# A transformer layer on one core: the last head's turn, the modulation sums and one row load get written places

## The chip, the cores and the metric

The kernel runs on one core of a Trainium2 chip. The metric is the device time of one execution in microseconds. A core has five engines that run side by side, each through its own list of instructions in order: TensorE (PE in the profile, matmuls into PSUM banks), VectorE (DVE), ScalarE (ACT), GpSimd (POOL) and SyncE (SP). Loads and stores are issued by SP and by ScalarE, each in the order of that engine's list.

## The reference

One layer of a hybrid decoder, for one sequence of 512 positions and 1024 channels, all in float32. A conditioning vector `c` gives six modulation vectors (`mod = silu(c) @ ada_w + ada_b`: shift, scale and gate of the mixer, and the same of the feed-forward part). What matters here is the end of the mixer and the start of the feed-forward part:

```python
h = rms_norm(h, ml_norm_g[l].reshape(H, Dh)).reshape(Bsz, S, D_ML)
h = (h * jax.nn.sigmoid(o_pre.astype(jnp.float32))).astype(x.dtype)
...
mix = jnp.concatenate([h, y], axis=-1) @ w_out[l]
x = x + g1 * rms_norm(mix, mix_post_g[l])
u = rms_norm(x, ffn_pre_g[l]) * (1.0 + sc2) + sh2
up = causal_dwconv(u @ ffn_up[l], ffn_conv_w[l], ffn_conv_b[l])
```

`h` are the outputs of four attention-like heads of 256 channels, `y` those of a convolution; `w_out` is the output projection, 2048 to 1024.

## The kernel before, in words

Channels are cut into tiles of 128 (one to a partition), the 512 positions into four tiles of 128. Every float32 product is made as three matmuls of split operands: a value is cut into a rounded part (`...h`) by a copy on ScalarE and a remainder (`...l`) by a subtraction on POOL (line 207, `w_split`; some on VectorE), and high x high, low x high and high x low are summed in PSUM (line 225, `mm3`). Weights come into two rotating buffers (`raws`), so the load of a weight waits until POOL has split the weight two loads earlier.

**The output projection** is done in two halves of 512 columns. The first half sums into the banks `mixa0` to `mixa3` (one for each position tile), the second into `mixb0` to `mixb3`. Three of the four heads go by a scheme of fewer products on 2 x 2 blocks (`mix_product`, with weight sums `mt1` to `mt4` and parts `m11`, `m21`, `m22`, and the results put together by VectorE: `mku`, and the updates of `mixb`); the ten pieces of `PLAIN` (the convolution's eight, and the last head's two as pieces 8 and 9) go directly (`wo0_n` for the first half, `wo1_n` for the second). The last head's outputs are turned (transposed on TensorE into `hT`), and split into `hh` by ScalarE (line 701) and `hl` by VectorE (line 702); pieces 8 and 9 need them.

**What sets the order.** TensorE and SP run in the order in which the program is written. On VectorE, ScalarE and POOL a scheduler orders the instructions by a model of time and by priority (`tc.cur_priority += LATER` makes a block less urgent), unless they stand in a block `with in_order()`, which keeps the three engines in written order, or unless one is tied behind another (`behind`, an order without a wait for data).

**The modulation sums.** `ada_block(i, ...)` loads row block i of the modulation weights (512 KB, `adaT`, issued on ScalarE) and sums its product with the condition on VectorE (line 189, `junk<-ada`, `junk<-wide` or `junk<-spare` by the buffer). I call them row i and sum i. Sums 16 to 23 give the gate of the mixer: `gain` makes the post-norm row from it, `send_rows` turns it on TensorE (`gT`), copies it (`gTs`, line 798) and writes it to DRAM (`row_d`, issued on ScalarE), and `row` loads it back into every partition (`wide<-row_d`, into the buffer that row 30 used before, issued on SP). Sums 24 to 39 give scale and shift of the feed-forward part.

**The chain behind the projection** (`chain_sums`, `chain_x`, `chain_u`), for each position tile: the sum of squares of both halves, `rm0t` on VectorE, a power on POOL, the new x, its squares, another power, the scaled `un`, and the transposes `xT` on TensorE, from which the first matmuls of the feed-forward part (`up`) get their operand. VectorE takes up the splits of the first up weight (`wup_0l` ... `wup_1536l`) just ahead of that.

## Time and profile before

| | us |
|---|---|
| median of the runs (three: 774.85, 775.5, 776.74) | 775.5 |
| the profiled execution | 776.75 |
| its span, first to last instruction | 775.0 |
| TensorE busy | 757.6 (98%) |
| VectorE busy | 580.1 (75%) |
| GpSimd busy | 547.3 (71%) |
| ScalarE busy | 427.7 (55%) |
| mean granted TensorE clock | 0.991 |

In the rows of a timeline the first number is the start in us from the start of the span, the second the time taken, then engine, line, operation and tiles (out<-in; the buffer numbers are left out, so `wo_8` stands for `wo0_8` and `wo1_8`). What stands in square brackets is the idle time of the engine before the instruction, and what ended it. A matmul's time covers its way through the array; what it costs TensorE is the distance to the next start.

### The profile page before, as it was taken

To read this page: it belongs to the slowest core of one execution; us is meant where nothing else is said; L and a number is where in the kernel's file an instruction comes from. 1 tells how busy PE (TensorE), PEld (TensorE's weight loads), DVE (VectorE), ACT (ScalarE), POOL (GpSimd) and SP (SyncE) were. 2 spreads that over 40 slices of the span, in tenths; PEclk is the share of its full clock that TensorE was granted. 3 is DMA by queue.
4 is the path that set the end of the run, shared out by engine and by line. 5 is a ranking of instruction groups with operands and counts; after the bars stand their busy time and mean duration, and the time that the engine had idled before them with its cause. 6 is when DMAs were issued, how large, how long until landed. Compare 5 with 4: busy or idle time off the path is not lost.

```text
span 775.0 us, 10264 instructions
## 1 busy us (share of the span) xinstructions
PE 757.6 (98%) x3485; PEld 626.6 (81%) x3485; DVE 580.1 (75%) x862; ACT 427.7 (55%) x823; POOL 547.3 (71%) x447
## 2 busy tenths in 40 slices
PE   7999999999999999999899999999999999999996
PEld 5878898878788788788678988888888888888885
DVE  6669999979689796488697878775765578654548
ACT  6675429784766656573347643443444345566633
POOL 5779849995685763858751066986988686599944
PEclk9999999999999999999899999999999999999999
DMA  8994954311140341855673755756586584896363
GB/s 316 343 389 160 184 148 129 128 70 56 54 135 30 126 170 45 278 208 206 230 257 126 246 222 184 295 229 236 206 303 227 185 295 157 298 397 244 105 239 141
DMA packets 41976, 154.92 MB, mean 200 GB/s; under 512 B 3954, under 2 KB 5378, under 8 KB 32772
## 3 DMA queue, kind: packets, MB, share of 16 engines
q1 hardware_dynamic: 28052, 101.57, 36.6%
q10 hardware_dynamic: 12272, 49.56, 17.6%
q0 software_dynamic: 1600, 3.15, 2.4%
q8 instruction: 27, 0.44, 0.2%
q14 instruction: 25, 0.20, 0.1%
HBM read 134.19 MB, written 26.35 MB: 207 GB/s over the span
## 4 chain that ended last, share of the span: by engine, by line
PE 87%; DVE 4%; DMA 3%; issue 2%; ACT 2%; POOL 1%; DVEq 0%; SPq 0%; POOLq 0%; ACTq 0%
PE up L225 31%; PE dn L225 13%; PE qko L225 13%; PE vo L225 8%; PE glu L225 7%; PE glu L362 4%; PE s L648 2%; PE o L659 2%; DVE junk L189 2%; PE v L225 1%; PE mixb L225 1%; DMA mt<-mixq 1%; PE mixa L225 1%; DMA wglu<-in_w_glu 1%; DMA wo<-in_w_out 1%
## 5 line engine op out<-in xcount | busy, mean ns | idle before, releaser
L911 DVE SCALAR_TENSOR_TENSOR cv<-gt,cvw,cv 128x502 f32<-128x502 f32 (+23 forms) x200 | 136.7, 729 | 2.7 <-ACT cv L899 1.6
L907 POOL TENSOR_TENSOR cs<-cs,cs 128x510 f32<-128x510 f32 (+3 forms) x32 | 41.9, 1308 | 1.3 <-ACT cs L905 1.0
L189 DVE SCALAR_TENSOR_TENSOR junk<-ada,cb 128x1024 bf16<-128x1024 f32 x21 | 35.6, 1696 | 5.9 <-DMA ada<-in_adaT 5.6
L207 POOL TENSOR_TENSOR wup_0l<-wup,wup_0h 128x512 fp32r<-128x512 f32 x18 | 26.0, 1444 | 17.2 <-ACT wup_0h L206 17.2
L225 PE MATMUL up<-u2h,wup_1024h 128*128 128x512 f32 (+1 forms) x96 | 35.8, 373 | 0.0
L225 PE MATMUL up<-u2h,wup_0h 128*128 128x512 f32 (+1 forms) x96 | 35.7, 372 | 0.0
L225 PE MATMUL up<-u2l,wup_512h 128*128 128x512 f32 (+1 forms) x96 | 35.7, 372 | 0.0
L225 PE MATMUL up<-u2l,wup_0h 128*128 128x512 f32 (+1 forms) x96 | 35.7, 372 | 0.0
L225 PE MATMUL up<-u2h,wup_0l 128*128 128x512 f32 (+1 forms) x96 | 35.7, 372 | 0.0
L225 PE MATMUL up<-u2h,wup_512l 128*128 128x512 f32 (+1 forms) x96 | 35.7, 371 | 0.0
L225 PE MATMUL up<-u2h,wup_1536l 128*128 128x512 f32 (+1 forms) x96 | 35.6, 371 | 0.0
L225 PE MATMUL up<-u2h,wup_1536h 128*128 128x512 f32 (+1 forms) x96 | 35.6, 371 | 0.0
L225 PE MATMUL up<-u2l,wup_1536h 128*128 128x512 f32 (+1 forms) x96 | 35.6, 371 | 0.0
L225 PE MATMUL up<-u2h,wup_512h 128*128 128x512 f32 (+1 forms) x96 | 35.6, 371 | 0.0
L225 PE MATMUL up<-u2l,wup_1024h 128*128 128x512 f32 (+1 forms) x96 | 35.6, 371 | 0.0
L225 PE MATMUL up<-u2h,wup_1024l 128*128 128x512 f32 (+1 forms) x96 | 35.6, 371 | 0.0
L905 ACT ACTIVATE cs<-gt,cvw 128x511 f32<-128x511 f32 (+4 forms) x40 | 27.0, 712 | 7.7 <-POOL cs L907 4.7
L207 POOL TENSOR_TENSOR wup_1536l<-wup,wup_1536h 128x512 fp32r<-128x512 f32 x18 | 24.2, 1347 | 7.5 <-ACT wup_1536h L206 7.0
L1383 POOL TENSOR_TENSOR b<-b 128x512 f32<-128x512 f32 x11 | 14.7, 1334 | 18.3 <-DVE b L1382 16.0
L342 DVE SCALAR_TENSOR_TENSOR junk<-ada,cps 128x1024 bf16<-128x1024 f32 x16 | 19.5, 1220 | 9.5 <-DMA ada<-in_adaT 8.7
L1384 DVE TENSOR_TENSOR b<-b 128x512 f32<-128x512 f32 x11 | 19.4, 1761 | 9.5 <-POOL b L1383 9.5
L207 POOL TENSOR_TENSOR wup_512l<-wup,wup_512h 128x512 fp32r<-128x512 f32 x18 | 25.3, 1403 | 0.0
(1263 smaller groups left out, 2785.6 us busy)
## 6 DMA issues: line engine op xcount, KB each, us to landing
wup<-in_w_up SPq DMA_DIRECT2D x22, 1024.0 KB, 5.4
b<-in_w_down ACTq DMA_DIRECT2D x11, 1024.0 KB, 7.1
spill_t<-b ACTq DMA_DIRECT2D x11, 1024.0 KB, 4.2
ada<-in_adaT ACTq DMA_DIRECT2D x21, 512.0 KB, 6.4
wqko<-in_w_qko SPq DMA_DIRECT2D x9, 1024.0 KB, 4.8
ada<-in_adaT SPq DMA_DIRECT2D x16, 512.0 KB, 7.3
wvo<-in_w_vo SPq DMA_DIRECT2D x6, 1024.0 KB, 4.8
wglu<-in_w_glu SPq DMA_DIRECT2D x5, 1024.0 KB, 8.9
```

The costliest lines, as they stand in the source:

```text
L189: t = V.scalar_tensor_tensor(out=junk, in0=r, scalar=1.0, in1=cb, op0=ALU.mult, op1=ALU.mult, accum_out=mod[:, i : i + 1])
L207: last_w[0] = (eng or G).tensor_tensor(out=lo[:, :n], in0=src, in1=hi[:, :n].bitcast(F32), op=ALU.subtract)
L225: PE.matmul(ps, l, r, start=start and i == 0, stop=stop and i == 2, skip_group_check=again)
L342: V.scalar_tensor_tensor(out=junk, in0=first[k][:, i * D : (i + 1) * D], scalar=1.0, in1=cps, op0=ALU.mult, op1=ALU.mult, accum_out=part[: ...
L362: PE.matmul(ps, blk(wk, i)[a], u[k][b], start=k == 0 and p == 0, stop=k == KT - 1 and p == 1)
L648: PE.matmul(sp[:, :n], ks[d][:, cc * P : (cc + 1) * P], qs[d][:, cc * P :], start=d == 0, stop=d == 1)
L659: PE.matmul(o[:, : DH + 2], E[h][cc][:, a : a + P], vs[h][cc], start=cc == 0, stop=cc == tt)
L905: S.activation(t[:, d:], cvx[j][:, : T - d], AF.Copy, scale=w(CK - 1 - d))
L907: G.tensor_tensor(out=side[:, d:], in0=side[:, d:], in1=t[:, d:], op=ALU.add)
L911: tap = V.scalar_tensor_tensor(out=cp[:, d:], in0=cvx[j][:, : T - d], scalar=w(CK - 1 - d), in1=cp[:, d:], op0=ALU.mult, op1=ALU.add)
L1383: G.tensor_tensor(out=b12, in0=b22, in1=b12, op=ALU.subtract)
L1384: V.tensor_tensor(out=b22, in0=b22, in1=b11, op=ALU.subtract)
```

## The change

The last steps of the last head (`for _ in steps`, transposes and `hh`, `hl`) move into the block in written order, behind the splits of `mt1` and of pieces 8 and 9 of the first half, and ahead of the split of `wo1_0`. `ada_block` is taken apart into `ada_load` and `ada_sum`. Sums 31 to 39, up to here placed by the scheduler behind `hl`, get written places in that block. Sums 27 to 30 are tied behind the copy `gTs`, not behind the last head's factors. The load `wide<-row_d` is written behind that of `wo1_0`.

```diff
-    def ada_block(i, behind, load_behind=None):
+    ada_rows = {}
+
+    def ada_load(i):
...
-        load = nc.scalar.dma_start(r, adaT[i // 2][:, (i % 2) * D : (i % 2 + 1) * D])
-        if load_behind is not None:
...
+        nc.scalar.dma_start(r, adaT[i // 2][:, (i % 2) * D : (i % 2 + 1) * D])
+        ada_rows[i] = r
+
+    def ada_sum(i):
         junk = small.tile([P, D], BF16, tag="junk", bufs=1, name=f"junk_{i}")
-        t = V.scalar_tensor_tensor(out=junk, in0=r, scalar=1.0, in1=cb, op0=ALU.mult, op1=ALU.mult, accum_out=mod[:, i : i + 1])
...
+        return V.scalar_tensor_tensor(out=junk, in0=ada_rows.pop(i), scalar=1.0, in1=cb, op0=ALU.mult, op1=ALU.mult, accum_out=mod[:, i : i + 1])
+
+    def ada_block(i, anchor):
+        ada_load(i)
+        behind(ada_sum(i), anchor)
...
-        V.tensor_copy(t[:n, :], ps[:n, :P])
+        last_sent[0] = V.tensor_copy(t[:n, :], ps[:n, :P])
...
-    for i in range(25, 31):
+    for i in range(25, 27):
         ada_block(i, last_e[0])
     tc.cur_priority -= LATER
     for n in range(1, 5):
         mix_first(n)
         if n == 4:
             send_rows(0, KT)
+            tc.cur_priority += LATER
+            for i in range(27, 31):
+                ada_block(i, last_sent[0])
+            tc.cur_priority -= LATER
     for n in range(5, NP - 2):
         mix_first(n)
         if n == 5:
             wt1 = right_load(mixq[1], "mt1")
             r8 = wo_load(NP - 2, 2)
-            g1r = row(0, lambda n: [wide1[:, :T], wide1[:, T : 2 * T]], "g1", nc.sync)
-    for _ in steps:
-        pass
-    tc.cur_priority += LATER
-    for i in range(31, 40):
-        ada_block(i, last_lo[0])
-    ada_done(24, 40)
-    tc.cur_priority -= LATER
...
+    for i in range(31, 38):
+        ada_load(i)
     with in_order():
         wt1 = right_split(wt1)
+        for i in range(2):
+            wo_split(r8, NP - 2, i)
+        for _ in steps:
+            pass
+        for i in range(31, 36):
+            ada_sum(i)
         for p in range(PAIRS):
             mix_product("s1", wt1, banks[:2], p, True)
-        for i in range(2):
-            wo_split(r8, NP - 2, i)
         for t, ps in zip(ku3, banks):
             V.tensor_tensor(out=t, in0=ps, in1=t, op=ALU.subtract)
         for t, ps in zip(ku2, banks):
             V.tensor_tensor(out=ps, in0=ps, in1=t, op=ALU.subtract)
-        we = wo1_split(wo1_load(0, EARLY), 0, EARLY)
+        ada_sum(36)
+        we = wo1_load(0, EARLY)
+        g1r = row(0, lambda n: [wide1[:, :T], wide1[:, T : 2 * T]], "g1", nc.sync)
+        we = wo1_split(we, 0, EARLY)
         w22 = right_split(right_load(w_mq[3], "m22"), slots, "t")
+        ada_load(39)
         for n in range(NP - 2, NP):
             mix_first(n)
...
+        ada_sum(37)
+        ada_load(38)
         for p in range(PAIRS):
             mix_product("s4", w22, banks[:2], p)
         for t, ps in zip(ku3, banks[2:]):
             V.tensor_tensor(out=ps, in0=ps, in1=t, op=ALU.add)
+        ada_sum(38)
+        ada_sum(39)
...
+    ada_done(24, 40)
```

The order on TensorE and on POOL stays as it was, instruction for instruction. Three places where it changes, each as it stands on the engine before and then with the change:

ScalarE, between the split of `mt1` and that of `m22`, before:

```order
L800 DMA row_d0_1429<-gTs0_3560 8x128
L206 ACTIVATE wo0_8h_3694<-wo0_8_3577 128x512
L206 ACTIVATE wo0_9h_3698<-wo0_8_3577 128x512
L206 ACTIVATE wo1_0h_3708<-wo1_0_3706 128x512
L206 ACTIVATE wo1_1h_3712<-wo1_0_3706 128x512
L701 ACTIVATE hh3_0_3610<-hT3_0_3605,ghalf_141 128x512
L701 ACTIVATE hh3_1_3619<-hT3_1_3614,ghalf_141 128x512
```

and with the change:

```order
L806 DMA row_d0_1429<-gTs0_3547 8x128
L210 ACTIVATE wo0_8h_3634<-wo0_8_3577 128x512
L210 ACTIVATE wo0_9h_3638<-wo0_8_3577 128x512
L705 ACTIVATE hh3_0_3647<-hT3_0_3642,ghalf_141 128x512
L705 ACTIVATE hh3_1_3656<-hT3_1_3651,ghalf_141 128x512
L210 ACTIVATE wo1_0h_3698<-wo1_0_3694 128x512
L210 ACTIVATE wo1_1h_3702<-wo1_0_3694 128x512
```

The two copies `hh` now stand ahead of the two splits of `wo1_0`. Further on, the load of row 38 moves on ScalarE from behind the first `wup` split to behind the squares of `mixa`, ahead of the splits of `wo1_6`.

VectorE, from the last head's remainders `hl` to the updates of `mixb`, before:

```order
L702 SCALAR_TENSOR_TENSOR hl3_1_3620<-hT3_1_3614,ghalf_141,hh3_1_3619 128x512
L189 SCALAR_TENSOR_TENSOR junk_31_3624,mod_139<-wide2_3452,cb_112 128x1024
L189 SCALAR_TENSOR_TENSOR junk_32_3627,mod_139<-spare_3101,cb_112 128x1024
L1152 TENSOR_TENSOR mku30_3334<-mixb0_3654,mku30_3334 128x512
L1152 TENSOR_TENSOR mku31_3335<-mixb1_3655,mku31_3335 128x512
L1154 TENSOR_TENSOR mixb0_3654<-mixb0_3654,mku20_3262 128x512
L1154 TENSOR_TENSOR mixb1_3655<-mixb1_3655,mku21_3263 128x512
L189 SCALAR_TENSOR_TENSOR junk_33_3630,mod_139<-spare_3101,cb_112 128x1024
```

and with the change:

```order
L706 SCALAR_TENSOR_TENSOR hl3_1_3657<-hT3_1_3651,ghalf_141,hh3_1_3656 128x512
L191 SCALAR_TENSOR_TENSOR junk_31_3660,mod_139<-wide2_3452,cb_112 128x1024
L191 SCALAR_TENSOR_TENSOR junk_32_3662,mod_139<-spare_3101,cb_112 128x1024
L191 SCALAR_TENSOR_TENSOR junk_33_3664,mod_139<-spare_3101,cb_112 128x1024
L191 SCALAR_TENSOR_TENSOR junk_34_3666,mod_139<-spare_3101,cb_112 128x1024
L191 SCALAR_TENSOR_TENSOR junk_35_3668,mod_139<-spare_3101,cb_112 128x1024
L1160 TENSOR_TENSOR mku30_3334<-mixb0_3603,mku30_3334 128x512
L1160 TENSOR_TENSOR mku31_3335<-mixb1_3604,mku31_3335 128x512
L1162 TENSOR_TENSOR mixb0_3603<-mixb0_3603,mku20_3262 128x512
L1162 TENSOR_TENSOR mixb1_3604<-mixb1_3604,mku21_3263 128x512
L191 SCALAR_TENSOR_TENSOR junk_36_3692,mod_139<-ada_36_3618,cb_112 128x1024
```

Five sums, not two, stand ahead of the updates that the s4 products wait for.

VectorE, the end of its list ahead of `rm0t`, before:

```order
L189 SCALAR_TENSOR_TENSOR junk_37_3644,mod_139<-ada_37_3642,cb_112 128x1024
L207 TENSOR_TENSOR wup0_0l_3853<-wup0_3850,wup0_0h_3852 128x512
L207 TENSOR_TENSOR wup0_512l_3857<-wup0_3850,wup0_512h_3856 128x512
L207 TENSOR_TENSOR wup0_1024l_3861<-wup0_3850,wup0_1024h_3860 128x512
L207 TENSOR_TENSOR wup0_1536l_3865<-wup0_3850,wup0_1536h_3864 128x512
L189 SCALAR_TENSOR_TENSOR junk_38_3648,mod_139<-ada_38_3646,cb_112 128x1024
L189 SCALAR_TENSOR_TENSOR junk_39_3651,mod_139<-wide2_3452,cb_112 128x1024
L194 TENSOR_TENSOR mod_139<-mod_139,vec_111 128x16
L1172 SCALAR_TENSOR_TENSOR gains_1428<-mod_139,vec_111 128x8
L1173 TENSOR_SCALAR gains_1428<-gains_1428 128x8
L828 TENSOR_SCALAR rm0t_3929<-msq_1441 128x1
```

and with the change:

```order
L1182 TENSOR_TENSOR mixb3_3606<-mixb3_3606,mku31_3335 128x512
L191 SCALAR_TENSOR_TENSOR junk_38_3811,mod_139<-ada_38_3789,cb_112 128x1024
L191 SCALAR_TENSOR_TENSOR junk_39_3813,mod_139<-wide2_3452,cb_112 128x1024
L198 TENSOR_TENSOR mod_139<-mod_139,vec_111 128x16
L1189 SCALAR_TENSOR_TENSOR gains_1428<-mod_139,vec_111 128x8
L1190 TENSOR_SCALAR gains_1428<-gains_1428 128x8
L211 TENSOR_TENSOR wup0_0l_3853<-wup0_3850,wup0_0h_3852 128x512
L211 TENSOR_TENSOR wup0_512l_3857<-wup0_3850,wup0_512h_3856 128x512
L211 TENSOR_TENSOR wup0_1024l_3861<-wup0_3850,wup0_1024h_3860 128x512
L211 TENSOR_TENSOR wup0_1536l_3865<-wup0_3850,wup0_1536h_3864 128x512
L834 TENSOR_SCALAR rm0t_3929<-msq_1441 128x1
```

The last two sums and the gains move ahead of the four splits of the first up weight. On SP one thing moves: the load of `wo1_0` stands ahead of the two of `wide<-row_d`, not behind them.

More of the change, by code (lines that the diff above doesn't have):

```diff
@@ L183, in ada_block @@
             r = adas.tile([P, D], F32, tag="ada", name=f"ada_{i}")
-        load = nc.scalar.dma_start(r, adaT[i // 2][:, (i % 2) * D : (i % 2 + 1) * D])
-        if load_behind is not None:
-            tc.add_manual_dep(load.ins, load_behind.ins.name, mybir.DependencyInfo(mybir.DependencyClass.NoSync, mybir.DependencyReason.DATA),
-                              reason="order on ScalarE")
+        nc.scalar.dma_start(r, adaT[i // 2][:, (i % 2) * D : (i % 2 + 1) * D])
+        ada_rows[i] = r
+    def ada_sum(i):
         junk = small.tile([P, D], BF16, tag="junk", bufs=1, name=f"junk_{i}")
-        t = V.scalar_tensor_tensor(out=junk, in0=r, scalar=1.0, in1=cb, op0=ALU.mult, op1=ALU.mult, accum_out=mod[:, i : i + 1])
-        tc.add_manual_dep(t.ins, behind.ins.name, mybir.DependencyInfo(mybir.DependencyClass.NoSync, mybir.DependencyReason.DATA),
-                          reason="order on VectorE")
+        return V.scalar_tensor_tensor(out=junk, in0=ada_rows.pop(i), scalar=1.0, in1=cb, op0=ALU.mult, op1=ALU.mult, accum_out=mod[:, i : i + 1])
+    def ada_block(i, anchor):
+        ada_load(i)
+        behind(ada_sum(i), anchor)
     def ada_done(a, b):
@@ L790, in decoder_layer @@
     rows_d = [dram.tile([D], F32, tag=f"row{i}", name=f"row_d{i}") for i in range(4)]
+    last_sent = [None]
     def send_rows(a, n, queue=nc.scalar):
```

## The prediction

> **What bounds the kernel now.** I read the page first (TensorE busy for 98% of the 775.0 us span, so only its pauses can be won back), then the chain of waits, whose last pieces are TensorE's own:
>
> ```profile
> 431.71 210.25 PE up L225 x984
> ```
>
> From 431.71 us to the end TensorE runs with next to no pause, so what the change does is worth the time by which that run starts sooner. Then I asked what TensorE waits for between 320 and 432 us:
>
> ```profile
> PE mixa L225 <- ACT hh L701: 3.5, 1, 3.5
> PE xT L1216 <- ACT un L1208: 2.1, 1, 2.1
> PE mixa L225 <- ACT mku L883: 0.2, 1, 0.2
> ```
>
> Two waits. The timeline of TensorE (start, us, what, idle before it and what ended that) shows each with its after-effect:
>
> ```profile
> 367.15 1.03 PE L691 MATMUL hT<-ident,hn 128*128 128x128 f32 x8
> 371.92 0.39 PE L225 MATMUL mixb<-mt_2h,ms 128*128 128x512 f32 x1
> ...
> 375.82 0.79 PE L225 MATMUL mixa<-wo_8h,hh 128*128 128x512 f32 x1 [3.51 <-ACT hh L701]
> ...
> 381.83 0.39 PE L225 MATMUL mixa<-wo_9h,hl 128*128 128x512 f32 x1
> ...
> 386.83 0.39 PE L225 MATMUL mixb<-m_0h,ms 128*128 128x512 f32 x1
> ...
> 390.92 0.39 PE L225 MATMUL mixb<-wo_0h,yh 128*128 128x512 f32 x1
> ...
> 405.65 0.39 PE L225 MATMUL mixb<-wo_3h,yl 128*128 128x512 f32 x1
> 408.13 1.23 PE L1216 MATMUL xT<-ident,un 128*128 128x128 f32 x8 [2.09 <-ACT un L1208]
> 409.01 0.78 PE L225 MATMUL mixb<-wo_4h,yh 128*128 128x512 f32 x1
> ...
> 412.48 0.39 PE L225 MATMUL mixb<-wo_6h,yl 128*128 128x512 f32 x1
> ```
>
> A 512-column matmul starts every 0.227 us (18 from 386.83 to 390.92). After the first wait the 14 matmuls from 375.82 to 381.83 (pieces 8 and 9) take 6.0 us instead of 3.2; after the second, the 8 from 409.01 to 412.48 take 3.5 instead of 1.8. The granted clock in one of these stretches:
>
> ```profile
> 378.00:379.00 1.00, 1.00 (x4) 0.71 (x4) 0.96 (x3) 0.00 (x0) 1.00 (x1) 0.50 0.68 106
> ```
>
> 0.50 is the clock. So the two waits cost 3.5 + 2.8 + 2.1 + 1.7 = 10.1 us, which is the most that can be won here. Who is late? ScalarE, the issues on SP, and the waits of SP's queue:
>
> ```profile
> 366.31 0.64 ACT L206 ACTIVATE wo_8h<-wo 128x512 fp32r<-128x512 f32 x1 [5.34 <-DVE gTs L798]
> 374.04 0.63 ACT L206 ACTIVATE wo_0h<-wo 128x512 fp32r<-128x512 f32 x1 [6.57 <-DMA wo<-in_w_out]
> 375.09 1.25 ACT L701 ACTIVATE hh<-hT,ghalf 128x512 fp32r<-128x512 f32 x2
> 367.74 0.80 SPq L806 DMA_DIRECT2D wide<-row_d  x2
> 368.65 0.36 SPq L1139 DMA_DIRECT2D wo<-in_w_out  x1
> SPq L806 <- DVE junk L189: 0.8, 1, 0.8
> ```
>
> The transposes of the last head are in at about 367.8 (half of the eight from 367.15), but the two `hh` copies stand on ScalarE behind the split of `wo1_0`, whose load was issued at 368.65, behind the two loads of the post-norm row. At 408.13 it is VectorE that is late: `rm0t`, the first step of the chain to `xT`, starts at 403.26, though the matmuls of its tile were over at 399.07, when those of tile 1 begin.
>
> ```profile
> 365.55 2.10 DVE L189 SCALAR_TENSOR_TENSOR junk<-wide,cb 128x1024 bf16<-128x1024 f32 x1
> ...
> 375.80 1.41 DVE L702 SCALAR_TENSOR_TENSOR hl<-hT,ghalf,hh 128x512 fp32r<-128x512 f32 x2 [8.13 <-ACT hh L701]
> 377.12 1.22 DVE L189 SCALAR_TENSOR_TENSOR junk<-wide,cb 128x1024 bf16<-128x1024 f32 x1
> 378.38 2.18 DVE L189 SCALAR_TENSOR_TENSOR junk<-spare,cb 128x1024 bf16<-128x1024 f32 x1
> 380.49 1.28 DVE L1152 TENSOR_TENSOR mku<-mixb,mku 128x512 f32<-128x512 f32 x2
> 381.69 1.28 DVE L1154 TENSOR_TENSOR mixb<-mixb,mku 128x512 f32<-128x512 f32 x2
> 399.07 0.39 PE L225 MATMUL mixb<-wo_2h,yh 128*128 128x512 f32 x1
> 402.77 0.17 DVE L194 TENSOR_TENSOR mod<-mod,vec 128x16 f32<-128x16 f32 x1
> 403.26 0.20 DVE L828 TENSOR_SCALAR rm0t<-msq 128x1 f32<-128x1 f32 x1
> ```
>
> A modulation sum on VectorE takes 1.22 us alone and 2.18 beside a POOL split; POOL's splits show the same two lengths, so the two take turns, 1.1 us each, 2.25 a pair:
>
> ```profile
> 368.75 1.29 POOL L207 TENSOR_TENSOR wo_9l<-wo,wo_9h 128x512 fp32r<-128x512 f32 x1
> 377.22 2.26 POOL L207 TENSOR_TENSOR m_0l<-m,m_0h 128x512 fp32r<-128x512 f32 x1
> 381.66 1.30 POOL L207 TENSOR_TENSOR m_2l<-m,m_2h 128x512 fp32r<-128x512 f32 x1
> ```
>
> Operations that read PSUM (`mku`, `mixb`, 0.6 us each) pass without such waits.
>
> **The change, part by part.** (1) *`hh` ahead of the `wo1_0` split.* ScalarE copies at 367.8 instead of 375.09. VectorE's `hl` follow; from the start of `hh` to the first sum behind `hl` it is 2.03 us (375.09 to 377.12), so that sum may start at 369.8. TensorE ends the s1 products at 372.15 and goes straight on to pieces 8 and 9 (`wo_9l` is there at 370.04): the 3.5 and the 2.8 us go.
>
> (2) *The row sent sooner, its load behind `wo1_0`.* The copy `gTs` moves from 365.4 to about 360, which ends ScalarE's 5.34 us wait. I cost this at nothing: POOL's `wo_8l` is held by sum 30 (365.55 and 2.10 us long) until 367.7 either way, and TensorE wants it at 372. The row's load waits last for that same sum (0.8 us in the queue's waits), so it doesn't start sooner. `wo1_0` does: its buffer is free when POOL ends `mt1_2l`, and that row and the landing times are
>
> ```profile
> 364.30 2.27 POOL L207 TENSOR_TENSOR mt_2l<-mt,mt_2h 128x512 fp32r<-128x512 f32 x1
> DMA to landing us min/median/max: 4.2/4.9/5.0
> DMA to landing us min/median/max: 4.0/6.7/9.2
> ```
>
> (first `wo`, then the `ada` rows). Issued at 366.6 instead of 368.65, `wo1_0` lands at about 371.2, `m22` (issued at 370.07 as now) by 375.
>
> (3) *Five sums ahead of the subtractions.* Before, two sums stood between `hl` and `mku`; now 31 to 35 do, with POOL's five splits between them. Sum 31 waits for `wo_9l` (370.04) and ends at 371.2, 32 at 372.4; then three pairs of 2.25: 374.6, 376.9, 379.15. The three `mku`/`mixb` operations up to tile 0's end at 381.0, all four at 381.6. TensorE is there at 372.15 + 36 x 0.227 = 380.3, so the s4 products wait 0.7 us: a new, small wait. Bounds: one turn of POOL less or more, 1.1 us, so no wait or 1.8 us, according to when `wo1_0` lands. All of TensorE's work is queued behind, but part 5 finds 2.9 us of slack there; even half speed behind this wait (2.8 us, as at 375.82) would vanish in it.
>
> (4) *The rest of VectorE's list.* `wo1_2` is issued at the end of `wo1_1l`, 375.8, lands at 380.8, and its first split is at POOL by 381.5, just ahead of sum 36, which ends at 383.95. Four `mg`: 386.4. Sum 37 behind a split: 388.7. Two `mixb`: 389.95. Now comes the only new wait on a load. The two rows on ScalarE:
>
> ```profile
> 389.01 0.60 ACT L821 ACTIVATE mixa3junk<-mixa 128x512 bf16<-128x512 f32 x1
> 394.86 0.34 ACTq L184 DMA_DIRECT2D ada<-in_adaT  x1
> ```
>
> Row 38, issued at 394.86 before, now goes out behind the last mixa square, which follows the last `mg` and with its accumulator takes 0.8 us: 387.2. By the median of 6.7 it lands at 393.9. POOL has its four last splits (`wo1_6`, issued at 381.5 behind `m22_2l`, has long landed) from 388.7 to 393.7 with VectorE out of the way. Sums 38 and 39 take 2.45, `mod` and the gains 0.5, four `wup` splits, now behind the sums, 4 x 0.6 = 2.4: `rm0t` at 399.2. From `rm0t` to `xT` the chain is 408.13 - 403.26 = 4.87 us, the same instructions: `xT` at 404.1.
>
> (5) *TensorE up to there.* From 381.0: s4 18, the early pieces 12 matmuls, 387.8; tile 0's 24, held by `wo_9l` (393.7) to 394.4; tile 1's 24, 399.8; six of tile 2, 401.2. It waits 2.9 us for `xT`, where it waited 2.09 before, so the half clock behind it stays (1.7 us, unchanged).
>
> **Sum.** `xT` moves from 408.13 to 404.1, 4.1 us; nothing behind it changes order. Of the 10.1 us that the waits cost, the rest goes to a longer second wait: VectorE gets 7.3 us earlier to its list (369.8 against 377.12) but spends 29.4 us on it instead of 26.1. Against the profiled run (776.75 us, its span 775.0 and 1.75 around it) that is 772.6; against the median of the runs shown, 775.5, it is **771.4 us**.
>
> **The rivals.** *A, the whole wait comes back:* VectorE isn't late, because row 38 lands by 391 and takes POOL's turns; then TensorE's 401.2 sets `xT`, 6.9 us sooner, and 768.6. For it: between two loads the DMA engines idle now (share 0.06 in the last but one column),
>
> ```profile
> 389.00:391.00 2.00, 2.00 (x11) 1.65 (x10) 2.00 (x1) 1.99 (x5) 1.70 (x2) 1.00 0.06 8
> ```
>
> so a row can come faster than the median. Against: VectorE's list must give up 2.9 us, and the lock-step with POOL gives no more than one or two turns of 1.1. 8%.
>
> *B, the clock:* `xT` as forecast, but full speed behind it: 1.7 us more, 769.7. Against it stands 408.13, where 2.09 us of idle time were enough for half speed: 8%. [...]
>
> *C, row 38 is late:* it is now issued 0.5 us ahead of `wup0` and the first x1 rows, not after they have landed. At the 9.2 us of the slowest such load it lands at 396.4, `rm0t` is at 401.7, `xT` at 406.6: 1.5 us sooner, 774.0, which is within 0.3%. [...] 20%.
>
> *D, slower:* the same place and mechanism further on. All of VectorE's list stands in order behind row 38, the squares and the gains of the second norm too, so each us past 393.8 is paid in full. It decides at 397.9 (10.7 us from issue to landing) between sooner and later than now, and beyond 400.2 (13 us) it is slower by over 0.3%, at 14 us it gives 778.8. No `ada` load took over 9.2. 5%.
>
> The change could also do nothing if `hh` were not what TensorE waits for; the row of 375.82 rules that out.
>
> **How the numbers follow.** The forecast has 59%, with 770.0 to 773.0 as its own range (one turn of 1.1 us either way in part 3 or 4). 0.3% is 2.3 us, about what a measurement can tell from no change. Faster by more: the forecast nearly whole, A and B, 0.73. Within: most of C and the edge of the forecast, 0.21. Slower: D and what I have not seen, 0.06. The range of 8 in 10 leaves out the best of A and D: 768.6 to 774.4.
>
> **What would show it.** Right: no wait of `mixa` on `hh`; `wo` issued before `wide` on SP, at 366.6; `hh` at 367.8; a wait of under 2 us ahead of the s4 products, ended by `mixb` on VectorE; `rm0t` between 398 and 401; a wait of 2 to 3.5 us ahead of `xT`, half speed behind it. Wrong: an `xT` that waits less than 1 us (A), full speed behind it (B), or VectorE idle for more than 4 us ahead of sum 38, ended by its load (C, D).

## The result

| | before | changed |
|---|---|---|
| median of the runs shown with the result, us | 775.5 (3 runs) | 770.21 (3 runs: 770.01 to 770.87) |
| ratio, with its 95% interval | | 0.9931 (0.9909 to 0.9954) |
| the same in a later comparison, us | 775.79 (8 runs) | 770.94 (5 runs), ratio 0.9935 (0.9921 to 0.9949) |
| span of the profiled execution, us | 775.0 | 768.5 |
| mean granted TensorE clock | 0.991 | 0.999 |

The change makes the kernel 5 us faster, 0.7%. The forecast was 771.4 us, in a range of 768.6 to 774.4. All eight runs of the changed kernel together have a median of 770.7 us (770.01 to 771.66); the experiments below are held against that.

Of the 6.5 us between the two profiled spans, 1.6 were there before the change's place: the transposes `hT` start at 367.15 before and at 365.57 now. So I count from `hT`. From the start of `hT` to the start of `xT` it was 408.13 - 367.15 = 40.98 us; now it is 36.07. The timeline of TensorE has the two places:

```profile
365.57 1.03 PE L695 MATMUL hT<-ident,hn 128*128 128x128 f32 x8
...
401.64 1.08 PE L1233 MATMUL xT<-ident,un 128*128 128x128 f32 x8
```

TensorE's last long run, in the chain of waits, starts at 425.19 in place of 431.71:

```profile
425.19 210.25 PE up L229 x984
```

From `xT` to the long run it is 23.6 us in both. So in these two executions the gain is 4.9 us between `hT` and `xT`, and nothing behind. What TensorE waits for between 320 and 426 us:

```profile
PE mixb L229 <- POOL wo_8l L211: 1.2, 1, 1.2
PE mixb L229 <- DVE mixb L1162: 0.7, 1, 0.7
PE mixb L229 <- POOL wo_7l L211: 0.5, 1, 0.5
PE up L229 <- ACT u2h L1255: 0.4, 1, 0.4
PE up L229 <- DVE u2l L1259: 0.3, 1, 0.3
PE mixb L229 <- POOL wo_9l L211: 0.3, 1, 0.3
PE xT L1233 <- ACT un L1225: 0.2, 1, 0.2
PE mixa L229 <- ACT mku L889: 0.2, 1, 0.2
```

The waits for `hh` (3.5) and for `un` (2.1, now 0.2) are gone and so are both stretches at half clock. What came instead are three short waits for POOL's splits of pieces 7, 8 and 9 (2.0 us) and the 0.7 us ahead of the s4 products. ScalarE and SP (timelines; `wo_0` is `wo1_0` here):

```profile
366.21 1.27 ACT L705 ACTIVATE hh<-hT,ghalf 128x512 fp32r<-128x512 f32 x2 [3.21 <-PE hT L695]
368.73 0.63 ACT L210 ACTIVATE wo_0h<-wo 128x512 fp32r<-128x512 f32 x1 [1.25 <-DMA wo<-in_w_out]
365.12 0.33 SPq L1141 DMA_DIRECT2D wo<-in_w_out  x1
366.26 0.80 SPq L812 DMA_DIRECT2D wide<-row_d  x2
```

VectorE's list ahead of the chain, the issue of row 38, and POOL's last splits:

```profile
383.99 0.33 ACTq L186 DMA_DIRECT2D ada<-in_adaT  x1
387.73 1.85 DVE L191 SCALAR_TENSOR_TENSOR junk<-ada,cb 128x1024 bf16<-128x1024 f32 x1 [1.80 <-DMA ada<-in_adaT]
389.63 2.18 DVE L191 SCALAR_TENSOR_TENSOR junk<-wide,cb 128x1024 bf16<-128x1024 f32 x1
391.85 1.12 DVE L198 TENSOR_TENSOR mod<-mod,vec 128x16 f32<-128x16 f32 x1
393.00 1.21 DVE L1189 SCALAR_TENSOR_TENSOR gains<-mod,vec 128x8 f32<-128x8 f32 x1
396.74 0.21 DVE L834 TENSOR_SCALAR rm0t<-msq 128x1 f32<-128x1 f32 x1
387.20 1.30 POOL L211 TENSOR_TENSOR wo_6l<-wo,wo_6h 128x512 fp32r<-128x512 f32 x1
388.46 2.27 POOL L211 TENSOR_TENSOR wo_7l<-wo,wo_7h 128x512 fp32r<-128x512 f32 x1
390.68 2.25 POOL L211 TENSOR_TENSOR wo_8l<-wo,wo_8h 128x512 fp32r<-128x512 f32 x1
392.89 1.29 POOL L211 TENSOR_TENSOR wo_9l<-wo,wo_9h 128x512 fp32r<-128x512 f32 x1
```

Row 38 lands 3.7 us after its issue. The sums 38 and 39 then meet POOL's splits and the taking of turns lengthens both sides: the sums take 1.85 and 2.18 us, two of the splits 2.27 and 2.25. TensorE (held by the splits) and VectorE (held by the sums) come to `xT` within 0.1 us of each other.

### The profile page after: what moved, and what is told of

Read it like the earlier page. It is cut to its first block, busy times and chain, and to the rows that moved or that the text cites. A ratio compares the mean times of both kernels' runs of the same rounds, so it can differ in the third digit from the quotient of the medians.

```text
span 768.5 us, 10263 instructions
## 1 busy us (share of the span) xinstructions
PE 754.3 (98%) x3485; PEld 623.0 (81%) x3485; DVE 580.0 (75%) x862; ACT 428.8 (56%) x823; POOL 547.7 (71%) x447
## 4 chain that ended last, share of the span: by engine, by line
PE 89%; DVE 4%; issue 2%; DMA 2%; ACT 1%; POOL 0%; DVEq 0%; SPq 0%; ACTq 0%; POOLq 0%
PE up L229 31%; PE dn L229 13%; PE qko L229 13%; PE vo L229 9%; PE glu L229 7%; PE mixa L229 5%; PE glu L366 4%; PE s L652 2%; PE o L663 2%; PE v L229 1%; DMA wglu<-in_w_glu 1%; DVE junk L191 1%; DMA xn<-in_x 1%; DMA ada<-in_adaT 0%; PE hT L695 0%
```

## The experiments

Times are medians; "over" and "under" are against the 770.7 us of the changed kernel. The last column is read from one profiled execution. Some of these kernels also take the code behind the block into the written order; in the traces of those that undo a part, each engine keeps the order of the changed kernel but for the places named.

| kernel | us (range) | ratio to before (95%) | from `hT` to `xT`, us |
|---|---|---|---|
| before | 775.8 | 1 | 40.98 |
| changed | 770.7 (770.0 to 771.7) | 0.9935 (0.9921 to 0.9949) | 36.07; 38.29 |
| part (1) alone, on before | 779.93 (777.5 to 782.1) | 1.0054 (1.0036 to 1.0072) | 45.94 |
| changed, part (1) undone | 770.98 (769.9 to 774.5) | 0.9949 (0.9930 to 0.9968) | 36.26 |
| changed, part (2) undone | 772.71 (771.2 to 774.7) | 0.9964 (0.9952 to 0.9977) | 39.39 |
| changed, parts (1) and (2) undone | 778.69 (777.4 to 779.4) | 1.0043 (1.0027 to 1.0060) | 43.78 |
| changed, end of part (4) undone | 776.8 (773.3 to 779.2) | 1.0018 (1.0001 to 1.0035) | 39.73 |
| changed, two sums ahead of `mku` | 772.52 (771.4 to 774.9) | 0.9958 (0.9943 to 0.9973) | 39.89 |
| changed, row 38 loaded early | 770.2 (769.1 to 772.7) | 0.9932 (0.9916 to 0.9948) | 35.86 |
| changed, `m22` loaded early | 772.21 (770.7 to 773.9) | 0.9952 (0.9934 to 0.9970) | 37.93 |
| changed, four sums left out | 768.51 (767.6 to 770.5) | 0.9919 (0.9903 to 0.9934) | 34.23 |
| changed, two sums behind the last split | 769.78 (769.1 to 771.3) | 0.9933 (0.9916 to 0.9949) | 35.13 |
| all places together | 768.44 (767.6 to 768.8) | 0.9902 (0.9884 to 0.9921) | 34.45 |

### Part (1) alone

On the kernel before; the other instructions are tied to their places of before.

```diff
         we = wo1_split(wo1_load(0, EARLY), 0, EARLY)
+        for i in range(EARLY):
+            behind(acts[f"wo1_{i}"], last_hh[0])
```

> The kernel before with part (1) alone: `hh` ahead of the `wo1_0` split on ScalarE; every other instruction on every engine keeps the order of before. Theory: TensorE's first wait (3.5 us) and the half clock behind it (2.8 us) go, but the VectorE list is only partly earlier. It starts 7 us sooner (`hl` follows `hh`), yet row 38 is still issued behind the first `wup0` split (about 393) and lands at about 397 to 400, so the sums 38 and 39 still end at 400 to 402.5 and `rm0t` comes at 400.3 to 403 in place of 403.26. TensorE, 5 to 6 us early, waits 3 to 6 us for `xT`, with a half clock behind it. Gain over before 0.5 to 3.0 us, so 772.5 to 775 us. Rival 1: part (1) is the whole change; then it gives the change's gain of 4.5 to 5.3 us (about 770.5) and no wait over 1 us stands at `xT`. Rival 2: the whole first wait comes back at `xT` and nothing is gained (775.5).

Measured: 4.1 us slower than before, where all three theories had it faster or equal. The first wait did go; the second became 8.7 us. Timelines of ScalarE's queue, VectorE and TensorE:

```profile
395.28 0.33 ACTq L184 DMA_DIRECT2D ada<-in_adaT  x1
403.85 1.23 DVE L189 SCALAR_TENSOR_TENSOR junk<-ada,cb 128x1024 bf16<-128x1024 f32 x1 [5.42 <-DMA ada<-in_adaT]
406.88 0.21 DVE L831 TENSOR_SCALAR rm0t<-msq 128x1 f32<-128x1 f32 x1
411.75 1.97 PE L1221 MATMUL xT<-ident,un 128*128 128x128 f32 x8 [8.71 <-ACT un L1213]
```

Row 38, issued at 395.28 behind the first `wup0` split, landed 8.6 us later. VectorE had been idle for 5.4 us by then. In the kernel before, sum 38 started without a wait 5.4 us behind the issue of its row (394.86, 400.24). There the next 1 MB load on SP, of the second up weight, went out 3.1 us behind row 38 (397.99); here, with POOL's splits done sooner, it goes out 0.2 us behind it (395.45). Whether that is what held the row isn't shown. So `hh` ahead of the split has no value by itself, and the landing of one load decides more than the whole of what I had added up.

### Part (1) undone

```diff
+        we = wo1_load(0, EARLY)
+        g1r = row(0, ..., "g1", nc.sync)
+        we = wo1_split(we, 0, EARLY)
         for _ in steps:
             pass
```

(and the same three lines taken out below.)

> The changed kernel with part (1) alone undone: the two pieces of `wo1_0` are split ahead of `hh` on ScalarE, all else as in the change (the `wo1_0` load is still sent at about 365.1). Theory: `wo1_0` lands at 368.7, so `hh` runs at 369.9 to 371.2 in place of 366.2 to 367.5; `hl` and the five sums behind it are 3.7 us later, of which VectorE's idle 1.8 us at row 38 takes a part. TensorE waits 1 to 2.5 us for `hh` or `hl`; the time is 1.5 to 4 us over the changed kernel (771.7 to 774.2). Rival 1: the whole wait and half clock return (3.5 + 2.8 us, 776.5). Rival 2: the time behind is set by GpSimd's splits, which do not move, and the cost is under 0.7 us (770.2 to 770.9).

Measured: 770.98 us, 0.3 over, which is no difference by the median; two of the six runs, at 773.3 and 774.5, are above every run of the changed kernel. In the profile, of a run of 770.55 us, ScalarE (first two rows) and TensorE:

```profile
367.52 0.64 ACT L210 ACTIVATE wo_0h<-wo 128x512 fp32r<-128x512 f32 x1 [4.36 <-DMA wo<-in_w_out]
368.58 1.25 ACT L705 ACTIVATE hh<-hT,ghalf 128x512 fp32r<-128x512 f32 x2
370.70 0.39 PE L229 MATMUL mixa<-wo_8h,hh 128*128 128x512 f32 x1
```

`wo1_0` had landed at 367.5, `hh` was done at 369.8, and TensorE wants it at 370.7. Where part (2) sends `wo1_0` early, `hh` is in time on either side of its split. The right rival was the second by its number, though for another reason than it gave: `hh`, 2.2 us later behind `hT` than in the change, wasn't late for TensorE. One difference is not of the edit: the load of `wo1_0` went out 1.8 us ahead of `hT` here (363.90) and 0.45 us ahead of it in both profiles of the changed kernel. What part (1) is worth with `wo1_0` as late as there isn't shown.

### Part (2) undone, and parts (1) and (2)

```diff
-    for i in range(25, 27):
+    for i in range(25, 31):
         ada_block(i, last_e[0])
...
-            for i in range(27, 31):
-                ada_block(i, last_sent[0])
...
-        we = wo1_load(0, EARLY)
         g1r = row(0, ..., "g1", nc.sync)
+        we = wo1_load(0, EARLY)
```

> The changed kernel with part (2) alone undone: the copy of `gTs` behind the sums 27 to 30, and the row load ahead of `wo1_0` on SyncE's queue; `hh` stays ahead of the `wo1_0` split. Theory (parts (1) and (2) each keep `hh` in time; with both undone it cost 8.5 us): `hh` runs at 366 as in the change and TensorE does not wait for it; `wo1_0` lands at about 372 in place of 368.7 and `m22` about 1 us later, so GpSimd's chain of splits ends 0 to 1 us later, while the sums 31 to 34 meet fewer splits: 0 to 1.5 us over the changed kernel (770.2 to 771.7), and from `hT` to `xT` 36 to 37.5 us (36.07 in the change). Rival (part (2) carries weight of its own, through the row send that holds ScalarE's queue and through `wo1_0`): 2.5 us or more over the changed kernel.

Measured: 772.71 us, 2.0 over; from `hT` to `xT` 39.39, outside what the theory gave. Part (2) has a weight of its own. ScalarE and POOL:

```profile
366.34 0.63 ACT L210 ACTIVATE wo_8h<-wo 128x512 fp32r<-128x512 f32 x1 [7.28 <-DVE gTs L804]
373.65 0.63 ACT L210 ACTIVATE wo_0h<-wo 128x512 fp32r<-128x512 f32 x1 [5.00 <-DMA wo<-in_w_out]
374.36 1.29 POOL L211 TENSOR_TENSOR wo_0l<-wo,wo_0h 128x512 fp32r<-128x512 f32 x1 [4.76 <-PE mixa L229]
```

The send of the row stands in ScalarE's list and waits for the late copy, so `wo_8h` starts at 366.34; `wo1_0` lands at 373.65 and POOL, idle for 4.8 us, ends its chain of splits 30.6 us behind `hT` in place of 28.6 (`wo_9l`). TensorE then waits for `wo_6l`, `wo_7l`, `wo_8l` and `wo_9l` (0.8, 0.3, 1.2 and 1.2 us). The second kernel also splits `wo1_0` ahead of `hh`:

> The changed kernel with parts (1) and (2) both undone: the copy of `gTs` behind the sums 27 to 30, the row load ahead of `wo1_0` on SyncE's queue, and the two pieces of `wo1_0` split ahead of `hh` on ScalarE. Undoing part (1) alone cost 0.8 us, because `wo1_0`, sent at 363.9, had landed at 367.5. Theory (part (1) is worth something only where `wo1_0` comes late, and either of the two parts suffices): `wo1_0` is sent at about 367.2 and lands at about 372, `hh` runs at 373.3, `hl` is ready at 375.8 in place of 368.3; TensorE waits 4 to 5 us for it, with a half clock behind, the sums 31 to 39 come 5 us later, and the time is 4 to 8 us over the changed kernel (774 to 778). Rival (the order hardly matters, VectorE's slack and the shared turns take it up): under 1.5 us over the changed kernel.

Measured: 778.69 us, 8.0 over, a little beyond the range. Waits of TensorE:

```profile
PE mixa L229 <- ACT hh L705: 3.5, 1, 3.5
PE mixb L229 <- DVE mixb L1161: 2.4, 1, 2.4
```

The wait for `hh` is back with its 3.5 us of before, and the five sums behind `hl` make the s4 products 2.4 us late as well. So each of the two parts keeps `hh` in time, and without both the written order is worse than the order of before.

### The end of part (4) undone

```diff
-        ada_load(38)
...
-        ada_sum(38)
-        ada_sum(39)
...
+        for a in range(0, 2048, T):
+            up_w[0].append(w_split(r[:, a : a + T], f"wup0_{a}", slots, "t", V))
+            if a == 0:
+                ada_load(38)
+        ada_sum(38)
+        ada_sum(39)
```

(The loop stands in place of one call of `w_load`, which makes the same four splits.)

> The changed kernel with the end of part (4) alone undone: the load of row 38 is issued behind the first `wup0` split on ScalarE, and the sums 38 and 39 and the gains stand behind the four `wup0` splits on VectorE, as before the change; all else as in the change. Theory (the run of part (1) alone: row 38 issued at 395.28 had landed only at 403.85, 8.6 us later, and TensorE waited 8.7 us for `xT`): the first `wup0` split runs at about 391.9, row 38 lands 3.7 to 8.6 us later, `rm0t` comes at 398.7 to 403.6 in place of 396.7, TensorE waits 2 to 7 us at `xT`, with a half clock behind a wait of over 2 us: 2 to 8.5 us over the changed kernel, 772 to 779 us. Rival (GpSimd's splits or TensorE set the end, the place of two sums does not matter): within 0.7 us of the changed kernel.

Measured: 776.8 us, 6.1 over, as the theory had it, and spread over 6 us. In the profiled execution, the fastest of them, the row landed 5.4 us after its issue (timelines of ScalarE's queue and of VectorE), and TensorE waited 5.5 us for `un` (waits):

```profile
391.45 0.34 ACTq L186 DMA_DIRECT2D ada<-in_adaT  x1
396.84 1.23 DVE L191 SCALAR_TENSOR_TENSOR junk<-ada,cb 128x1024 bf16<-128x1024 f32 x1 [2.24 <-DMA ada<-in_adaT]
```

```profile
PE xT L1239 <- ACT un L1231: 5.5, 1, 5.5
```

This place alone is worth more than the whole change brings.

### Fewer sums ahead of the subtractions

```diff
-        for i in range(31, 36):
+        for i in range(31, 33):
             ada_sum(i)
...
-        ada_sum(36)
+        for i in range(33, 37):
+            ada_sum(i)
```

> The changed kernel with part (3) thinned: two sums (31 and 32) instead of five ahead of the `mku` and `mixb` subtractions, the sums 33 to 36 behind them. Theory: the subtractions end at about 374.4 in place of 379.9 and TensorE's wait of 0.7 us ahead of `s4` goes, but the four sums then stand ahead of the `mg` products, which come at about 382.6 in place of 381.1; the squares behind them and the load of row 38 on ScalarE are 1.5 us later, `rm0t` is 1 to 3 us later, and TensorE waits 1 to 3 us at `xT`: 0 to 2.5 us over the changed kernel. Rival (the wait ahead of `s4` was a loss of the change): 0.7 us under the changed kernel.

Measured: 772.52 us, 1.8 over, in the range, but not where I had put it. The wait ahead of s4 is gone, and the `mg` products come at 384.0. At `xT` TensorE does not wait; it is late itself. With four sums beside them POOL's eleven splits from `m_0l` to `wo_9l` take 20.7 us (375.02 to 395.69) in place of 19.0, and TensorE waits five times for them, 0.3 to 1.2 us each and 3.6 in all.

### What sets the end: row 38 early, `m22` early

My first reading of the result was that GpSimd's chain of splits sets TensorE's arrival and that VectorE is level with it by chance.

```diff
-        if 20 <= i < 24 or 32 <= i < 36:
-            q = 2 * (i % 4)
+        if 20 <= i < 24 or 32 <= i < 36 or i == 38:
+            q = 2 * (i % 4) if i < 38 else 0
...
+        ada_load(38)
         ada_load(39)
...
-        ada_load(38)
```

> The changed kernel with row block 38 put into the free first quarter of the `spare` tile and its load issued with that of row 39 behind the `m22` splits (about 375) in place of 384; nothing else changes its order. VectorE's 1.8 us wait for row 38 goes. Theory (TensorE's arrival at `xT` is set by GpSimd's splits of the last `wo` pieces, VectorE ends level with it by chance): `rm0t` comes 1 to 1.8 us sooner, TensorE still reaches `xT` at the same time behind `wo_9l`, and the time stays within 0.7 us of the changed kernel. Rival (VectorE's list sets the end, as the prediction had it): 1.0 to 1.8 us faster than the changed kernel, about 768.8.

Measured: 770.2 us, no difference, as the theory said. But `rm0t` came only 0.4 us sooner, not 1 to 1.8: sum 38, begun 1.9 us sooner, took 2.36 us, and `mod` and the two gains behind it 1.1 to 1.2 us each.

```diff
             r8 = wo_load(NP - 2, 2)
+            m22 = side("m22")
+            nc.sync.dma_start(m22[:, : PAIRS * T], w_mq[3])
...
-        w22 = right_split(right_load(w_mq[3], "m22"), slots, "t")
+        w22 = right_split((m22, "m22"), slots, "t")
```

> The changed kernel with the `m22` weights loaded early into a tile of the side pool, ahead of `wo1_0` on SyncE's queue; orders on the other engines unchanged. It frees one of the two raw buffers, so the later `wo` and `wup0` loads are sent sooner too. Theory (GpSimd's chain of splits from `m22` on sets TensorE's arrival at `xT`): GpSimd's idle 2.1 us ahead of `m_0l` goes, `wo_9l` ends 1.5 to 2.1 us sooner, TensorE's waits of 0.5, 1.2 and 0.3 us for `wo_7l`, `wo_8l` and `wo_9l` shrink by as much, and the time is 1.0 to 2.0 us under the changed kernel (768.2 to 769.2). Rival (VectorE's list sets the end): the splits end sooner, TensorE waits 1 to 2 us at `xT` for `un` instead, and the time is within 0.5 us of the changed kernel.

Measured: 772.21 us, 1.5 over, where the theory had 1 to 2 under. The six runs fall into two groups, three at 770.7 to 771.0 us and three at 773.4 to 773.9; the profile is of one of the slower three (773.72), so what follows is shown for them. POOL's pause ahead of `m_0l` did go, and VectorE paid for it: each of the sums 31 to 35 took 2.2 us, `mku` came 13.9 us behind `hT` in place of 12.0, and the load of row 38, which waits for the squares behind it, went out at 388.64. It landed at 394.74. Waits of TensorE:

```profile
PE mixb L229 <- DVE mixb L1164: 2.6, 1, 2.6
PE xT L1236 <- ACT un L1228: 2.5, 1, 2.5
```

So the theory fell in this form. My reading from here on: a pause of one of the two engines is time in which the other runs at full pace (alone a sum takes 1.2 us and a split 1.3, and either can take 2.2 to 2.4 beside the other), and what counts is the work of both together. The next two kernels test it.

### The turns tested: four sums left out, two sums behind the last split

```diff
-        ada_sum(36)
...
-        ada_sum(37)
...
-        ada_sum(38)
-        ada_sum(39)
```

> The changed kernel without VectorE's sums 36, 37, 38 and 39 (their rows are still loaded; the four columns of `mod` are set to zero, so this part of the modulation is left out). Theory (VectorE's operations on two operands in SBUF and GpSimd's splits take turns: a sum of 1.2 us or a split of 1.3 us takes 2.2 to 2.3 us when it meets the other, so that the two engines together set the end): the splits behind take 1.3 us each, `wo_9l` ends at 392.1 in place of 394.2 (the last four pieces land at 386.5 as now), `rm0t` comes at 395.0 behind the `wup0` splits, and the time is 1.5 to 2.0 us under the changed kernel (768.2 to 768.7). Rival (the longer splits have another cause, or the end is set by transfers): `wo_9l` ends at 394 as now and the time is within 0.5 us of the changed kernel.

Measured: 768.51 us, 2.2 under, 34.23 us from `hT` to `xT`. POOL's timeline:

```profile
386.48 1.29 POOL L212 TENSOR_TENSOR wo_6l<-wo,wo_6h 128x512 fp32r<-128x512 f32 x1 [2.30 <-ACT wo_6h L211]
390.25 1.28 POOL L212 TENSOR_TENSOR wo_9l<-wo,wo_9h 128x512 fp32r<-128x512 f32 x1
```

The four splits follow each other at 1.25 us, and `wo_9l` ends 26.7 us behind `hT`, 1.9 sooner. With the sums gone the splits are short: that is the turns.

```diff
-        ada_sum(38)
-        ada_sum(39)
...
+        r6 = wo1_load(EARLY + 4, NP)
+        wo += wo1_split(r6, EARLY + 4, NP)
+        ada_sum(38, r6[:, 2 * T : 4 * T])
+        ada_sum(39)
...
-        r = chain_x(0, r)
+        r = chain_x(0, r, low0)
+        low0()
```

(`low0` does the next of the four `wup0` subtractions on VectorE; two more stand further down in the chain.)

> The changed kernel with less taking of turns: sum 38 writes its unused products into the buffer of the last four `wo` pieces, so that the sums 38 and 39 come behind GpSimd's last split; and the four `wup0` splits of VectorE, which are first read at about 413, stand in the gaps of the chain behind `rm0t` instead of ahead of it. Nothing is left out. Theory (turns): `wo_7l`, `wo_8l` and `wo_9l` take 1.3 us each and `wo_9l` ends at 392.1 to 392.3, the sums 38 and 39 run at 1.2 us each behind it, `rm0t` comes at 395.3 in place of 396.7, TensorE reaches `xT` at 399.7 and waits 0.3 to 0.6 us there: 1.0 to 1.7 us under the changed kernel (768.5 to 769.2). Rival: the end is not set by the turns but by transfers or by TensorE's own work, and the time is within 0.5 us; or the splits moved into the chain make it longer, up to 1 us over the changed kernel.

Measured: 769.78 us, 0.9 under, with ranges that overlap, so the times don't settle it. The profile shows the mechanism (its `hT` starts 1.3 us later than that of the first profile of the changed kernel):

```profile
392.51 1.27 POOL L212 TENSOR_TENSOR wo_9l<-wo,wo_9h 128x512 fp32r<-128x512 f32 x1
393.82 1.23 DVE L192 SCALAR_TENSOR_TENSOR wo<-ada,cb 128x1024 f32<-128x1024 f32 x1 [6.55 <-POOL wo_9l L212]
396.72 0.21 DVE L835 TENSOR_SCALAR rm0t<-msq 128x1 f32<-128x1 f32 x1
```

VectorE leaves 6.6 us unused, the splits and then the sums run at full pace, and the end comes no later than with both at work all the time: 35.13 us from `hT` to `xT`, 0.9 less than the shorter of the changed kernel's two.

### All places together

```diff
+            m22 = side("m22")
+            nc.sync.dma_start(m22[:, : PAIRS * T], w_mq[3])
...
-        for i in range(31, 36):
+        for i in range(31, 33):
             ada_sum(i)
...
+        ada_sum(33)
+        ada_sum(34)
...
+        ada_load(38)
         ada_load(39)
...
+        r6 = wo1_load(EARLY + 4, NP)
+        wo += wo1_split(r6, EARLY + 4, NP)
         for tt, ps in enumerate(mixa):
```

> An attempt at a kernel faster than both; nothing is left out. It takes the run with sum 38 behind GpSimd's last split and the `wup0` splits in the gaps of the chain (from `hT` to `xT` 35.1 us there, 36.07 in the change), and adds: `m22` loaded early into the side pool, so that GpSimd's splits start without their idle 2 to 3 us and the last `wo` pieces are sent sooner; row 38 loaded with row 39 behind the `m22` splits; two sums ahead of `mku`, two behind `mixb`, two behind `mg`, sum 37 behind the second `mixb` additions; and the splits of the last four `wo` pieces ahead of the squares of `mixa` on ScalarE. Theory (the turns between VectorE and GpSimd set the end, and these places spread them): `wo_9l` ends 2 to 3 us sooner than in that run, no wait over 1 us is left on TensorE, from `hT` to `xT` 33.2 to 34.5 us, and the time is 1.5 to 2.8 us under the changed kernel (767.4 to 768.7). Rival (GpSimd's splits without a pause lengthen VectorE's sums and make the subtractions late again, as they did where `m22` alone came early): a wait of 1 to 3 us ahead of `s4` or at `xT` and no gain, 770 to 772.

Measured: 768.44 us (767.63 to 768.76), 2.3 under the changed kernel (none of its eight runs is below 770.01) and 1.0% under the kernel before. From `hT` to `xT` it is 34.45 us; TensorE's longest wait there is 0.6 us, for `un`:

```profile
390.71 1.27 POOL L212 TENSOR_TENSOR wo_9l<-wo,wo_9h 128x512 fp32r<-128x512 f32 x1
394.92 0.21 DVE L835 TENSOR_SCALAR rm0t<-msq 128x1 f32<-128x1 f32 x1
400.18 1.09 PE L1254 MATMUL xT<-ident,un 128*128 128x128 f32 x8 [0.61 <-ACT un L1246]
```

`m22` early and fewer sums ahead of `mku`, with medians 1.5 and 1.8 us over by themselves, are both part of the fastest kernel here.

### The changed kernel once more

> The changed kernel itself, once more and in more rounds, as the base of the comparisons with it: the runs that undo or add one part differ from it by 0.4 to 8.5 us, and its own median (770.21 us) rests on 3 runs. Theory (these differences are of the kernels, not of the occasion): a median within 0.8 us of 770.21, a ratio to the kernel before of 0.992 to 0.994, from `hT` to `xT` 35.8 to 36.4 us in the profiled execution, with no wait over 1.3 us on TensorE between them. Rival (the time varies from one occasion to the next by more than that): a median over 771.5 or under 769, which would leave the differences under 2 us open.

Measured: the median is as expected (770.94), the profile isn't: 38.29 us from `hT` to `xT` in an execution of 771.66 us, the slowest of the eight. TensorE's waits, and its clock behind them (in a table by stage the clock is the third number from the end):

```profile
390.59 0.50 PE L229 MATMUL mixb<-wo_6l,yh 128*128 128x512 f32 x1 [0.85 <-POOL wo_6l L211]
392.80 0.50 PE L229 MATMUL mixb<-wo_7l,yh 128*128 128x512 f32 x1 [1.24 <-POOL wo_7l L211]
395.01 0.80 PE L229 MATMUL mixb<-wo_8l,hh 128*128 128x512 f32 x1 [1.25 <-POOL wo_8l L211]
396.00:398.00 2.00, 2.00 (x6) 1.48 (x5) 1.97 (x5) 0.39 (x1) 0.19 (x1) 0.50 0.26 57
```

Counted from `hT`, the last `wo` load landed 1.4 us later than in the other execution and row 38 1.2 us later; the turns fell differently, and half clock came on top. So the changed kernel runs in more than one pattern, and the last column of the table, one execution each, is good to about 2 us.

Behind `xT` part of this comes back (the first row from the timeline of TensorE, the second from the chain of waits):

```profile
404.57 1.03 PE L1233 MATMUL xT<-ident,un 128*128 128x128 f32 x8
426.63 210.25 PE up L229 x984
```

From `xT` to the long run it is 22.1 us here, not 23.6. In two more profiles TensorE came late to `xT` by its own waits for POOL's splits (part (2) undone, two sums ahead of `mku`); there it is 22.0 us, so for these three the last column shows some 1.5 us too much. In all the others it is 23.2 to 23.6 us, with half clock behind `xT` (before, part (1) alone, end of part (4) undone, `m22` early) and without.

## Why the prediction was right, and where it was wrong

**The first wait goes: right in effect, wrong in its credit.** `hh` runs when `hT` is there, and the 3.5 and 2.8 us are gone. The prediction gave this to part (1). Undoing part (1) costs nothing by the median; undoing (2) costs 2.0 us, undoing both 8.0. Part (2) it put down at nothing ("I cost this at nothing"), but for `wo1_0` issued 2 us sooner; the step that failed there took ScalarE's wait for the copy and POOL's wait for `wo1_0` for harmless. `wo1_0` was issued at 365.12, 366.7 in before's time (366.6 forecast).

**Part (3): right.** The s4 products wait 0.7 us, the number forecast (in the second profile they don't wait).

**Part (4): the right place, with a size that is luck.** `rm0t` was forecast at 399.2; it came at 396.74, 398.3 in before's time. Row 38 went out 1.6 us sooner than forecast (383.99, 385.6 in before's time, against 387.2), because sums 36 and 37 took 1.21 us each, ahead of the splits that they met; and it took 3.7 us, not 6.7. But VectorE did not gain those 4.6 us: the sums 38 and 39, `mod` and the gains, which I had put down at their short lengths because POOL would be through by then, took turns with POOL's last splits (6.5 us, 387.73 to 394.2, in place of 2.95). This part is what the change stands on: with it undone the kernel is no faster than before, and with part (1) alone it is slower, by the mechanism of rival D, VectorE's list stuck behind row 38.

**Part (5): wrong.** I had TensorE at `xT`'s place at 401.2 and 2.9 us of waiting there, with a half clock behind. It came at 403.2 in before's time and waited for nothing. The term that was mis-sized is POOL's last four splits: 5.0 us forecast "with VectorE out of the way", 7.0 measured (387.20 to 394.18), because an early row 38 is an early contender. So `wo_9l` came at 395.8 in before's time in place of 393.7, and TensorE came later by the same 2 us. That the sums are the cause shows where they come late: with the end of part (4) undone the four splits take 1.28 to 1.29 us each and `wo_9l` ends 26.7 us behind `hT`, not 28.6. By the prediction's own signs of being wrong (an `xT` that waits less than 1 us, full speed behind it) its account of the end fails. That the time came so close is luck: VectorE lost in the turns most of what row 38 gained, and TensorE, 2 us late, met it there. That such short waits left the clock whole in one profiled execution and not in the other wasn't foreseen.

**The sum** came out 0.8 to 1.2 us short: 4.1 us forecast, 4.9 in the profile, 4.8 to 5.3 in the medians. In the profile `xT` is 0.9 us sooner than forecast, and the 1.65 us of half clock behind it, which rival B priced at 1.7, are gone without a gain: from `xT` to the long run it is 23.6 us with it and without it. Waits of 0.2, 0.4 and 0.3 us stand in its place in the changed kernel (for `un`, `u2h` and `u2l`); by the distances between TensorE's starts there they cost 1.3 us over its pace, and the other 0.3 to 0.4 us I can't place. So here it was the steps behind on VectorE and ScalarE that set the stretch. In the second profile, where TensorE came to `xT` 2.2 us later behind `hT`, it met no such wait and the stretch was 22.1 us.

**The rivals.** A's time (768.6) was reached only by kernels that also took away or spread POOL's turns. C's delay is real (3.7 to 8.6 us from issue to landing where sum 38 waited for it) and may be what spreads the run with the end of part (4) undone, of which one execution was profiled; in the change the row goes out early enough that it mostly doesn't show. D's "No `ada` load took over 9.2" holds for the stretch from 310 to 432 us that it was read from; over the whole kernel before, the slowest took 13.8 us, so D's 5% rested on too short a stretch.

The turns are what the prediction read from two lengths and then applied only where it saw both engines busy. In the changed kernel a split of 1.29 us takes 2.25 to 2.27 beside the sums 38 and 39, and a split beside an operation that reads PSUM stayed short (`m_2l`, 1.30 us at 381.66 in the prediction's rows, beside `mixb` at 381.69). Why the two engines take turns these runs don't show.

## What to carry to other kernels

Where two engines take turns at something, add up the work of both over the stretch and ask what must be done first; an idle engine may be what lets the other finish (here VectorE's 6.6 us without work, in which POOL's last four splits took 1.27 to 1.30 us each). When an instruction list in order waits for a load, the issue of that load is the place to look at: here one load and two sums, placed some 8 us sooner, are worth more than the whole change. And before crediting an edit, undo it alone and together with its neighbours: of two parts that each remove the same wait, neither shows it one by one.

## What the runs showed of the hardware

Small operations took turns as well. `mod` (128x16) and the gains (128x8) took 0.17 us each before the change, alone; beside POOL's splits they take 1.12 and 1.21 us.

The clock fell on waits that were short one by one. In the second profile of the changed kernel waits of 0.85, 1.24 and 1.25 us within 4.4 us brought it to 0.50 for some 3 us; in the first, 0.51, 1.25 and 0.28 us left it at 1.00. In the run with two sums ahead of `mku`, waits of 0.81, 0.29, 0.28 and 1.24 us within 4.7 us came ahead of half clock and one of 0.97 us fell within it; it lasted longer there (a table by stage):

```profile
394.00:400.00 6.00, 5.03 (x13) 3.49 (x12) 5.33 (x12) 2.76 (x6) 2.23 (x2) 0.50 0.67 245
```

None of these waits is longer than 1.25 us, and matmuls ran between them. What the clock goes by these runs don't show.

Where sum 38 waited for it, the 512 KB load of row 38 took between 3.7 us (changed kernel) and 8.6 us (part (1) alone) from issue to landing, and 5.9 us in another execution of the same changed kernel. In the two experiments in which it was sent behind the first `wup0` split, with the same loads sent right behind it, it took 8.6 and 5.4 us; what decides between them these runs don't show.
